# A decoder layer on one core: the next unit's projection cut into six pieces that follow the attention's stages, and four bias tiles

## The chip, the cores and the metric

The kernel runs on one core of a Trainium2 chip. The core has a matrix engine (PE; the weight loads that precede its matmuls are a row of their own, PEld), a vector engine (DVE), a scalar engine (ACT) and GpSimd (POOL), each with its own instruction stream that is worked off in order; SP issues DMAs. The metric is the device time of one execution in microseconds, the median of several runs. The engines' streams are laid out ahead of time by a tile scheduler: it goes through the program as written and by priorities, puts the instructions in an order on each engine, and adds the semaphore waits.

## The reference

A layer with two kinds of attention heads on one normed input, one output projection and an MLP; sequence and model width 1024, batch 1:

```python
def token_mixer(h, ...):
    proj = h @ w_in                       # q, k, v of 4 differential heads (2 x 64) and 8 FoX heads (64), f_logit
    cum = jnp.cumsum(jax.nn.log_sigmoid(f_logit), axis=1)
    def block(args):
        ...
        sd = q.k * 64**-0.5 + t5_bias(distance)      # differential: two score maps per head
        pd = softmax(where(causal, sd, NEG))
        ad = pd[:, :, 0] - lam * pd[:, :, 1]
        od = rmsnorm(ad @ dv, subln_g) * (1.0 - lambda_init)
        sf = q.k * 64**-0.5 + cum_q - cum_k          # FoX
        of = softmax(where(causal, sf, NEG)) @ fv
        return concatenate([od, of])
def reference(x, ...):
    h = rmsnorm(x, ln_attn_pre)
    x = x + rmsnorm(token_mixer(h, ...) @ w_out, ln_attn_post)
    u = square(relu(rmsnorm(x, ln_mlp_pre) @ w_up))
    return x + rmsnorm(u @ w_down, ln_mlp_post)
```

The code above is cut and in short form; all is float32.

## The kernel before, in words

Float32 products are made of rounded parts: each operand is split into a high part (`hi`, a cast on ACT) and a low part (`lo`, the difference, on DVE or POOL), and three matmuls (hi by hi, hi by lo, lo by hi) add up in one accumulation.

*Startup.* The eight 128-row tiles of x are loaded, and `norm_transposed` (L88 to L102) norms each: a Square on ACT (L90) into a tile y, a reciprocal root (`rstd_of`, L74 to L85), a multiplication on DVE into y (L92), eight transposes on PE (L98), the high part by ACT (L100, `hh`) and the low part by DVE (L101, `hl`). The tile y has the name "bias" and two slots in all, which it shares with the attention's bias tiles; unit 0's bias is loaded into one of them at the sixth turn of the loop.

*Units.* The attention is done in eight units u: 0 to 3 are the differential heads, 4 to 7 pairs of FoX heads. `unit_project(u)` makes the unit's q, k and v. `load_w` (L113) fetches one of the three weights (128 columns, a DMA on SP), casts it on ACT (L70, `whi`) and subtracts on POOL (L71, `wlo`), two slots each. `project` (L239) does a piece of 512 rows of h: 24 matmuls (L243 to L245) into a PSUM tile "dense" (two slots), then evacuates it at high priority: q by ACT and DVE (L261, L262), k by ACT, DVE and copies between partitions on SP (L269 to L273), v by ACT (L276), four transposes on PE (L280) and high and low part `vv` on ACT and DVE (L283, L284; FoX L289, L290). A unit has three weights and two such pieces of each. Unit 0 is done in 256-row pieces between its attention's stages.

*Attention.* `unit_attention(u, ms, ...)` goes through stages: for a differential unit m = 0 to 3, for a FoX unit m = 0 to 3 with either head, thus 4 or 8 of growing width. A stage is `softmax` (L309): scores on PE (L323, mask L326 for FoX, L328), bias and row maximum in one DVE reduction (L332), exp on ACT (L338), reciprocal on DVE (L341), and the scaling, on DVE for differential heads (L346 to L348), on POOL for FoX (L352). Then `flush` issues the `attend` of the stage before: transposes of the probabilities (L379), high and low part (ACT L381, DVE L382), V matmuls (L390 to L394; FoX L398, L399), for differential heads a norm with a matmul by ones (L409), and a store to DRAM (L424).

*Order.* The main loop (L484) writes for each u: the whole `unit_project(u)`, then `bias_tiles(u)` (a 512 KB DMA; FoX units have two), then `unit_attention(u)`. Unit 7's projection is written between unit 6's m = 1 and m = 2; `split_w_out` (eight casts and subtractions of the output projection's weight, POOL L71 `wol`) and unit 7's attention follow. The scheduler mixes what is written one behind the other: the next unit's matmuls fill places of the attention before. A period in what follows is the time from one unit's first attend to the next unit's.

Of the kernel before, what the change touches and what calls it, by code (L numbers as in the profile page):

```python
# [16 lines left out]
P = 128  # L17
# [16 lines left out]
def layer_kernel(ctx, tc, x, ln_attn_pre, w_in, b_f, lam_q1, lam_k1, lam_q2, lam_k2, subln_g,  # L34
# [111 lines left out]
    def bias_tiles(u):  # L146
        if u < 4:
            tb = bp.tile([P, S], F32, name="bias", bufs=2)
            nc.sync.dma_start(tb, toeplitz(u))
            return [tb, tb]  # L150
        tiles = []
        for s in range(2):
            tb = bp.tile([P, S], F32, name="bias", bufs=2)
            nc.sync.dma_start(tb, cumd[2 * (u - 4) + s].partition_broadcast(P))
            tiles.append(tb)
        return tiles
# [7 lines left out]
    for t in range(NB + 1):  # L164
# [19 lines left out]
        if t:  # L184
            y = bp.tile([P, D], F32, name="bias", bufs=2)
            norm_transposed(xts[t - 1], g_pre, y, hh, hl, t - 1)
# [61 lines left out]

    def unit_project(u):
        diff = u < 4  # L250
        base = 128 * u if diff else 1536 + 128 * (u - 4)
        qs = [b1.tile([P, S], F32R, name=f"qs{s}") for s in range(2)]
        k1 = [b1.tile([P, S], F32R, name=f"k1{s}") for s in range(2)]
        kl = [bp.tile([P, S], F32R, name=f"kl{s}") for s in range(2)]
        vt = b1.tile([P, S], F32, name="vt", bufs=1)
        vv = bp.tile([P, NB, 256], F32R, name="vv")

# [17 lines left out]
        def evac_v(ps, cs):  # L275
            nc.scalar.copy(vt[:, cs], ps)  # L276
            t0, nt = cs.start // P, (cs.stop - cs.start) // P
            tr = ps_t.tile([P, 4, P], F32, name="tr")[:, :nt, :]
            for k in range(nt):
                nc.tensor.transpose(tr[:, k, :], vt[:, (t0 + k) * P:(t0 + k + 1) * P], ident)  # L280
            dst = vv[:, t0:t0 + nt, :]
# [11 lines left out]
        evacs = (evac_q, evac_k, evac_v)  # L293
        if u == 0:
            for c in range(4):
                for w, evac in zip(w_first, evacs):
                    project(w, evac, c, 256)
                if c == 0:
                    lam_setup()
                    tiles = (qs, k1, kl, vv, bias0)  # L300
                unit_attention(0, (c,), *tiles)
        else:
            for n, evac in enumerate(evacs):
                w = load_w(base + 512 * n)
                for c in range(2):
                    project(w, evac, c, 512)
        return qs, k1, kl, vv

# [49 lines left out]
    def attend(u, m, heads, vv, probs):  # L358
# [6 lines left out]
        for kp in range(m + 1):  # L365
# [18 lines left out]
            for n, k in enumerate(order):  # L384
# [4 lines left out]
                if diff:  # L389
                    nc.tensor.matmul(pv[:, 0, :], vv[:, k, 0:128], rh, start=start,  # L390
                                     stop=False)
                    nc.tensor.matmul(pv[:, 0, :], vv[:, k, 0:128], rl, start=False,
                                     stop=False)
                    nc.tensor.matmul(pv[:, 0, :], vv[:, k, 128:256], rh, start=False,  # L394
                                     stop=stop)
                else:
                    vs = vv[:, k, 128 * s:128 * s + 128]
                    nc.tensor.matmul(pv[:, s, :], vs, rh, start=start, stop=False)  # L398
# [37 lines left out]

    def unit_attention(u, ms, qs, k1, kl, vv, bias):
        for u, m, heads in stages(u, ms):
            probs = softmax(u, m, heads, qs, k1, kl, vv, bias)
            flush()  # L440
            waiting.append(lambda u=u, m=m, heads=heads, probs=probs: attend(u, m, heads, vv, probs))

# [40 lines left out]
    octx = ExitStack()  # L483
    for u in range(8):  # L484
        if u == 1:
            forget_gates()
        if u == 7:
            unit_attention(6, range(2), *tiles)
        proj = unit_project(u)
        if u == 7:  # L490
            hctx.close()
            wo = pool("wo", stack=octx, side="right")
            w_o = []
            unit_attention(6, (2,), *tiles)
            split_w_out(0)
            unit_attention(6, (3,), *tiles)
            split_w_out(4)
        if u == 0:
            continue
        tiles = (*proj, bias_tiles(u))  # L500
        if u == 6:
            continue
        unit_attention(u, range(4), *tiles)
    flush()
# [433 lines left out]
```

## Time and profile before

| | |
|---|---|
| median of 3 runs | 1255.13 us (1254.7 to 1255.17) |
| profiled execution's own time | 1255.45 us |
| its span | 1253.7 us |
| PE busy | 1217.9 us, 97% of the span |
| PEld busy | 1009.0 us, 80% |
| DVE, ACT, POOL busy | 865.5 (69%), 647.7 (52%), 167.8 us (13%) |
| the chain that ended last, by engine | PE 87%, DVE 5%, ACT 4%, POOL 2%, DMA 2% |
| granted PE clock | 1.00 in every stretch read |

Busy time of PE counts a matmul from its start to its modelled end; matmuls overlap, so a stretch can be 100% busy and still hold waits between starts. An engine's row in a grouped view gives how many instructions, their busy time, the mean of one, and the idle time ahead of them with what ended it.

### The profile page before, as it was taken

To read this page: it belongs to the slowest core of one execution; us is meant where nothing else is said; L and a number is where in the kernel's file an instruction comes from. 1 tells how busy PE (TensorE), PEld (TensorE's weight loads), DVE (VectorE), ACT (ScalarE), POOL (GpSimd) and SP (SyncE) were. 2 spreads that over 40 slices of the span, in tenths; PEclk is the share of its full clock that TensorE was granted. 3 is DMA by queue.
4 is the path that set the end of the run, shared out by engine and by line. 5 is a ranking of instruction groups with operands and counts; after the bars stand their busy time and mean duration, and the time that the engine had idled before them with its cause. 6 is when DMAs were issued, how large, how long until landed. Compare 5 with 4: busy or idle time off the path is not lost.

```text
span 1253.7 us, 17424 instructions
## 1 busy us (share of the span) xinstructions
PE 1217.9 (97%) x6076; PEld 1009.0 (80%) x6076; DVE 865.5 (69%) x1844; ACT 647.7 (52%) x1269; POOL 167.8 (13%) x248
## 2 busy tenths in 40 slices
PE   6899999999999998999999999999999999999997
PEld 5877888888888887788887888888888888888886
DVE  6893969695747427855588667666645784775998
ACT  5663646464646438745474554454444444444552
POOL 3011111102323218400001000000000000000100
PEclk9999999999999999999999999999999999999999
DMA  7423031312131325333404544435349963335474
GB/s 244 115 73 85 26 97 39 93 56 63 52 88 48 84 59 193 102 127 115 150 18 126 210 157 171 146 134 182 120 158 345 365 193 95 101 93 168 147 230 170
DMA packets 122524, 164.15 MB, mean 131 GB/s; under 512 B 9656, under 2 KB 80312, under 8 KB 120516
## 3 DMA queue, kind: packets, MB, share of 16 engines
q1 hardware_dynamic: 116436, 130.53, 34.6%
q0 software_dynamic: 5424, 31.46, 6.2%
q8 instruction: 48, 0.79, 0.3%
q10 hardware_dynamic: 576, 1.05, 0.2%
q14 instruction: 40, 0.33, 0.1%
HBM read 112.62 MB, written 44.35 MB: 125 GB/s over the span
## 4 chain that ended last, share of the span: by engine, by line
PE 87%; DVE 5%; ACT 4%; POOL 2%; DMA 2%; issue 1%; SPq 0%; DVEq 0%; ACTq 0%; POOLq 0%
PE dense L244 6%; PE dense L245 6%; PE dense L243 6%; PE sc L575 3%; PE sc L577 3%; PE sc L579 3%; PE tr L379 3%; PE tr L779 3%; PE tr L780 3%; PE tr L781 3%; PE dense L780 2%; PE dense L781 2%; PE tr L575 2%; PE tr L577 2%; PE dense L779 2%; PE sc L779 2%
## 5 line engine op out<-in xcount | busy, mean ns | idle before, releaser
L70 ACT CAST whi<-wraw 128x512 fp32r<-128x512 f32 (+4 forms) x167 | 126.5, 763 | 263.2 <-PE dense L244 59.0
L71 DVE TENSOR_TENSOR wlo<-wraw,whi 128x512 fp32r<-128x512 f32 (+4 forms) x144 | 116.1, 808 | 92.1 <-ACT whi L70 86.8
L243 PE MATMUL dense<-hh,whi 128*128 128x512 f32 (+1 forms) x400 | 151.2, 378 | 1.8 <-DVE qs L262 1.3
L245 PE MATMUL dense<-hh,wlo 128*128 128x512 f32 (+1 forms) x400 | 152.4, 381 | 0.0
L244 PE MATMUL dense<-hl,whi 128*128 128x512 f32 (+1 forms) x400 | 151.7, 379 | 0.1
L338 ACT ACTIVATE p<-p,nmax 128x128 f32<-128x128 f32 (+7 forms) x128 | 99.4, 778 | 30.5 <-DVE nmax L332 28.7
L332 DVE CUSTOM_DVE_ANT_0 p<-sc,bias 128x512 f32<-128x512 f32 (+3 forms) x128 | 74.2, 585 | 38.0 <-PE sc L328 30.3
L71 POOL TENSOR_TENSOR wlo<-wraw,whi 128x1024 fp32r<-128x1024 f32 x23 | 55.5, 2412 | 241.8 <-ACT whi L70 188.4
L243 PEld LDWEIGHTS dense<-hh,whi 128*128 128x128 f32 x400 | 76.2, 191 | 14.2 <-issue 1.7
L244 PEld LDWEIGHTS dense<-hl,whi 128*128 128x128 f32 x400 | 76.1, 190 | 12.4 <-DVE hl L101 0.4
L245 PEld LDWEIGHTS dense<-hh,wlo 128*128 128x128 f32 x400 | 76.1, 190 | 11.1
L382 DVE TENSOR_TENSOR pl<-tr,ph 128x512 fp32r<-128x512 f32 (+1 forms) x120 | 73.5, 630 | 9.0 <-ACT ph L381 6.1
L379 PE MATMUL tr<-ident,p 128*128 128x128 f32 x432 | 67.7, 274 | 7.6 <-POOL p L352 5.4
L323 PE MATMUL sc<-k,qs 128*128 128x512 f32 (+2 forms) x192 | 73.2, 383 | 1.3 <-DVE nmax L332 1.2
L381 ACT CAST ph<-tr 128x512 fp32r<-128x512 f32 (+1 forms) x120 | 61.9, 543 | 21.9 <-PE tr L379 16.6
L328 PE MATMUL sc<-kl,qs 128*128 128x512 f32 (+2 forms) x192 | 71.7, 376 | 1.4 <-DMA kl<-kl 1.4
L379 PEld LDWEIGHTS tr<-ident,p 128*128 128x128 f32 x432 | 50.8, 140 | 15.6 <-POOL p L352 8.0
L614 DVE TENSOR_TENSOR r<-sc,m 128x512 f32<-128x512 f32 x42 | 28.9, 689 | 40.0 <-PE sc L579 40.0
L352 POOL TENSOR_SCALAR p<-p,rs 128x128 f32<-128x128 f32 (+3 forms) x64 | 49.3, 775 | 50.3 <-DVE rs L341 43.0
L779 PE MATMUL tr<-whi 128*128 128x512 f32 x144 | 56.0, 389 | 0.0
L780 PE MATMUL tr<-wlo,whi 128*128 128x512 f32 x144 | 56.0, 389 | 0.0
L781 PE MATMUL tr<-whi,wlo 128*128 128x512 f32 x144 | 56.0, 389 | 0.0
(293 smaller groups left out, 3241.7 us busy)
## 6 DMA issues: line engine op xcount, KB each, us to landing
wraw<-ud SPq DMA_DIRECT2D x112, 256.0 KB, 2.8
ud<-sp POOLq DMA_DIRECT2D x15, 1024.0 KB, 4.6
b<-in_w_down_dram SPq DMA_DIRECT2D x48, 256.0 KB, 5.4
wraw<-in_w_in_dram SPq DMA_DIRECT2D x23, 512.0 KB, 4.1
ud<-r POOLq DMA_DIRECT2D x15, 768.0 KB, 5.2
wraw<-in_w_down_dram SPq DMA_DIRECT2D x36, 256.0 KB, 4.1
wraw<-in_w_up_dram SPq DMA_DIRECT2D x16, 512.0 KB, 4.2
k<-in_w_up_dram SPq DMA_DIRECT2D x16, 512.0 KB, 4.9
```

What stands on the lines that cost most here:

```text
L70: nc.scalar.copy(hi, src)
L71: (lo_eng or nc.vector).tensor_tensor(lo, src, hi.bitcast(F32), op=ALU.subtract)
L243: nc.tensor.matmul(ps, hi[:, kt, :], hh[:, kt, cs], start=kt == 0, stop=False)
L244: nc.tensor.matmul(ps, hi[:, kt, :], hl[:, kt, cs], start=False, stop=False)
L245: nc.tensor.matmul(ps, lo[:, kt, :], hh[:, kt, cs], start=False, stop=kt == KT - 1)
L332: nc.vector.tensor_tensor_reduce(out=pr[:, c0:c1], in0=sc[:, :c1 - c0], in1=bias[s][:, b0 + c0:b0 + c1], scale=-1.0, scalar=BIG if nmax is ...
L338: nc.scalar.activation(pr[:, :w], pr[:, :w], AF.Exp, bias=nmax, scale=-1.0, accum_out=ssum)
L379: nc.tensor.transpose(tr[:, first + n, :], probs[i][:, k * P:(k + 1) * P], ident)
L382: nc.vector.tensor_tensor(pl[:, first:], tr[:, first:], ph[:, first:].bitcast(F32), op=ALU.subtract)
L779: nc.tensor.matmul(ps[k], sh[:, cs], th, start=p == 0, stop=False)
L780: nc.tensor.matmul(ps[k], sh[:, cs], tl, start=False, stop=False)
L781: nc.tensor.matmul(ps[k], sl[:, cs], th, start=False, stop=p == NP - 1)
```

## The change

`unit_project(u)` no longer does the work for u from 1 on; it returns the tiles (lists that are filled when a piece is first issued) and six pieces: q, k, v by two halves of 512 rows. `unit_attention` takes these pieces and a count for each of its stages, and writes so many of them behind the `flush` of the stage. Unit u + 1's pieces are written in unit u's attention: for the differential units 1 to 3 with the counts 1, 1, 2, 2; for the FoX units 4 and 5 with 0, 1, 0, 1, 1, 1, 1, 1; unit 7's in the first four stages of unit 6 (m = 0 and 1) with 1, 1, 2, 2. Unit 1's own pieces follow the forget gates in one row, as before. The bias tiles of unit u + 1 are loaded ahead of unit u's attention, and "bias" has four slots. The two further tiles of 128 x 1024 float32 take 8 KiB of each partition; the program's scratch for dynamic DMAs is set to 8192 bytes.

```diff
     def bias_tiles(u):
         if u < 4:
-            tb = bp.tile([P, S], F32, name="bias", bufs=2)
+            tb = bp.tile([P, S], F32, name="bias", bufs=4)
...
         if t:
-            y = bp.tile([P, D], F32, name="bias", bufs=2)
+            y = bp.tile([P, D], F32, name="bias", bufs=4)
             norm_transposed(xts[t - 1], g_pre, y, hh, hl, t - 1)
...
         else:
-            for n, evac in enumerate(evacs):
-                w = load_w(base + 512 * n)
-                for c in range(2):
-                    project(w, evac, c, 512)
-        return qs, k1, kl, vv
+            ws = {}
+
+            def piece(n, c):
+                if c == 0:
+                    tiles_of(n)
+                    ws[n] = load_w(base + 512 * n)
+                project(ws[n], evacs[n], c, 512)
+
+            pieces = [lambda n=n, c=c: piece(n, c) for n in range(3) for c in range(2)]
+        return tiles, pieces
...
-    def unit_attention(u, ms, qs, k1, kl, vv, bias):
-        for u, m, heads in stages(u, ms):
+    def unit_attention(u, ms, qs, k1, kl, vv, bias, fill=(), counts=()):
+
+        fill = list(fill)
+        for (u, m, heads), n in zip(stages(u, ms), counts or [0] * 8):
             probs = softmax(u, m, heads, qs, k1, kl, vv, bias)
             flush()
+            for _ in range(n):
+                fill.pop(0)()
             waiting.append(lambda u=u, m=m, heads=heads, probs=probs: attend(u, m, heads, vv, probs))
...
-    for u in range(8):
-        if u == 1:
-            forget_gates()
-        if u == 7:
-            unit_attention(6, range(2), *tiles)
-        proj = unit_project(u)
...
-        tiles = (*proj, bias_tiles(u))
-        if u == 6:
-            continue
-        unit_attention(u, range(4), *tiles)
+    unit_project(0)
+    forget_gates()
+    proj, pieces = unit_project(1)
+    for piece in pieces:
+        piece()
+    tiles = (*proj, bias_tiles(1))
+    for u in range(1, 6):
+        proj, pieces = unit_project(u + 1)
+        bias = bias_tiles(u + 1)
+        unit_attention(u, range(4), *tiles, pieces,
+                       (1, 1, 2, 2) if u < 4 else (0, 1, 0, 1, 1, 1, 1, 1))
+        tiles = (*proj, bias)
+    proj, pieces = unit_project(7)
+    bias = bias_tiles(7)
+    unit_attention(6, range(2), *tiles, pieces, (1, 1, 2, 2))
...
+    unit_attention(7, range(4), *proj, bias)
...
-    nc = bacc.Bacc("TRN2", target_bir_lowering=False, num_devices=1)
+    nc = bacc.Bacc("TRN2", target_bir_lowering=False, num_devices=1,
+                   dynamic_dma_scratch_size=8192)
```

The order of the instructions at three places. First ACT in the startup, before; `bias` here is the tile y, and L90 is its Square:

```order
30 L100 CAST hh<-tr 128x4x128 x2
31 L90 ACTIVATE bias,ssq<-p 128x1024
32 L78 ACTIVATE rs_r<-ssq,eps 128x1
33 L202 ACTIVATE lam_s<-lam_s 128x2
34 L81 ACTIVATE rs_r<-rs_r 128x1
35 L338 ACTIVATE p,ssum<-p,nmax 128x256
36 L269 CAST k_419<-dense 64x256
37 L269 CAST k_420<-dense 64x256
38 L100 CAST hh<-tr 128x4x128 x2
39 L90 ACTIVATE bias,ssq<-p 128x1024
40 L276 COPY vt<-dense 128x256
41 L78 ACTIVATE rs_r<-ssq,eps 128x1
```

and after the change, where the line numbers below L180 are the same and the later ones stand 7 to 15 higher:

```order
28 L90 ACTIVATE bias,ssq<-p 128x1024
29 L268 ACTIVATE qs_417<-dense 64x256
30 L78 ACTIVATE rs_r<-ssq,eps 128x1 x2
31 L81 ACTIVATE rs_r<-rs_r 128x1 x2
32 L268 ACTIVATE qs_418<-dense 64x256
33 L100 CAST hh<-tr 128x4x128 x2
34 L90 ACTIVATE bias,ssq<-p 128x1024
35 L276 CAST k_419<-dense 64x256
36 L78 ACTIVATE rs_r<-ssq,eps 128x1
37 L81 ACTIVATE rs_r<-rs_r 128x1
38 L276 CAST k_420<-dense 64x256
39 L100 CAST hh<-tr 128x4x128 x3
```

The Squares (L90) of the last rows of x now follow one another closely, ahead of unit 0's first exps (L338 before, L353 now).

Second, ACT at the change from unit 1's attention to unit 2's, before; the k, vt and vv rows evacuate unit 2's pieces, exp (L338) of 128x128 is unit 2's first stage:

```order
195 L407 ACTIVATE tmp<-pv 128x256
196 L410 ACTIVATE dr<-tr,eps 128x256
197 L411 ACTIVATE dr<-dr 128x256
198 L70 CAST whi<-wraw 128x1024
199 L269 CAST k_2572<-dense 64x512
200 L269 CAST k_2573<-dense 64x512
201 L276 COPY vt<-dense 128x512
202 L283 CAST vv<-tr 128x4x128
203 L70 CAST whi<-wraw 128x1024
204 L276 COPY vt<-dense 128x512
205 L338 ACTIVATE p,ssum<-p,nmax 128x128 x2
206 L283 CAST vv<-tr 128x4x128
```

and after (L283 is vt, L290 vv, L353 exp, L396 ph, L422 to L426 the norm):

```order
191 L396 CAST ph<-tr 128x384
192 L353 ACTIVATE p,ssum<-p,nmax 128x896
193 L353 ACTIVATE p,ssum<-p,nmax 128x1024 x2
194 L422 ACTIVATE tmp<-pv 128x256
195 L283 COPY vt<-dense 128x512
196 L425 ACTIVATE dr<-tr,eps 128x256
197 L426 ACTIVATE dr<-dr 128x256
198 L290 CAST vv<-tr 128x4x128
199 L70 CAST whi<-wraw 128x1024
200 L283 COPY vt<-dense 128x512
201 L353 ACTIVATE p,ssum<-p,nmax 128x128 x2
202 L290 CAST vv<-tr 128x4x128
```

The k evacuations and the first half of v's have moved ahead of or among the last exps and the norm of unit 1; the last four rows, from the cast of the next weight over vt and the exps to vv, stand as before.

Third, POOL between two FoX units, before; L352 is the scaling of the probabilities, L373 and L374 clear two blocks, L71 is the low part of a projection weight:

```order
76 L352 TENSOR_SCALAR p<-p,rs 128x896
77 L352 TENSOR_SCALAR p<-p,rs 128x1024
78 L373 MEMSET ph 128x128
79 L374 MEMSET pl 128x128
80 L71 TENSOR_TENSOR wlo<-wraw,whi 128x1024 x3
81 L352 TENSOR_SCALAR p<-p,rs 128x128
82 L352 TENSOR_SCALAR p<-p,rs 128x256
83 L352 TENSOR_SCALAR p<-p,rs 128x128
84 L373 MEMSET ph 128x128
```

and after, where L367 is the scaling, within one unit's stages:

```order
69 L71 TENSOR_TENSOR wlo<-wraw,whi 128x1024
70 L388 MEMSET ph 128x128
71 L389 MEMSET pl 128x128
72 L367 TENSOR_SCALAR p<-p,rs 128x640
73 L367 TENSOR_SCALAR p<-p,rs 128x768
74 L388 MEMSET ph 128x128
75 L367 TENSOR_SCALAR p<-p,rs 128x640
76 L389 MEMSET pl 128x128
77 L367 TENSOR_SCALAR p<-p,rs 128x768
78 L71 TENSOR_TENSOR wlo<-wraw,whi 128x1024
79 L367 TENSOR_SCALAR p<-p,rs 128x896
```

The three subtractions that stood together behind a unit's widest scalings now stand apart, each between scalings of that unit.

## Rows read from the trace of the kernel before

**Rows 1.** Page, busy us of each engine (share of the span), instructions
```profile
PE 1217.9 (97%) x6076; PEld 1009.0 (80%) x6076; DVE 865.5 (69%) x1844; ACT 647.7 (52%) x1269; POOL 167.8 (13%) x248
```

**Rows 2.** Windows: stretch, length, busy PE, PEld, DVE, ACT, POOL (instructions), PEclk, DMA
```profile
15.00:76.00 61.00, 56.40 (x414) 52.15 (x414) 50.17 (x142) 37.05 (x97) 9.17 (x8) 1.00 0.46 135
...
187.10:244.70 57.60, 56.91 (x304) 47.44 (x305) 44.88 (x129) 31.88 (x70) 8.58 (x11) 1.00 0.24 65
...
365.50:429.20 63.70, 63.58 (x370) 53.38 (x369) 36.76 (x104) 35.28 (x78) 21.64 (x36) 1.00 0.25 67
429.20:471.00 41.80, 41.44 (x216) 34.41 (x215) 16.93 (x41) 16.91 (x40) 9.12 (x18) 1.00 0.22 57
471.00:522.00 51.00, 44.52 (x290) 36.04 (x289) 38.31 (x120) 41.09 (x87) 36.77 (x45) 1.00 0.45 147
```

**Rows 3.** Chain of waits: start us, length us, what held the end
```profile
179.77 0.23 PE dense L245
...
182.28 0.24 PE dense L244
...
182.59 1.05 ACT whi L70
...
186.44 0.61 DVE vv L284
...
187.09 0.66 PE tr L379 x4
...
189.26 0.12 PE pv L390
...
194.72 0.43 PE tr L409 x2
...
301.04 0.06 PE sc L326
```

**Rows 4.** PE grouped by shape, 187.0 to 244.6: busy, mean ns, idle before
```profile
L245 PE MATMUL dense<-hh,wlo 128*128 128x512 f32 x48 | 19.4, 404 | 0.0
...
L379 PE MATMUL tr<-ident,p 128*128 128x128 f32 x36 | 5.4, 274 | 0.7 <-DVE vv L284 0.7
```

**Rows 5.** PE grouped by shape, 365.5 to 429.2
```profile
L326 PE MATMUL sc<-mask_b,ident_b 128*128 128x128 bf16 x16 | 3.7, 229 | 0.0
```

**Rows 6.** Windows, the halves of two periods and two stretches of the startup
```profile
182.60:215.00 32.40, 31.71 (x184) 26.70 (x183) 30.23 (x98) 22.33 (x52) 6.19 (x10) 1.00 0.09 26
215.00:240.20 25.20, 25.20 (x123) 20.75 (x124) 14.66 (x31) 9.55 (x18) 2.39 (x1) 1.00 0.44 115
358.00:397.00 39.00, 38.88 (x253) 32.81 (x252) 29.24 (x92) 26.66 (x64) 15.33 (x30) 1.00 0.18 55
397.00:421.00 24.00, 24.00 (x116) 20.10 (x115) 7.52 (x12) 8.07 (x14) 6.34 (x6) 1.00 0.34 84
30.00:45.00 15.00, 12.36 (x99) 11.62 (x98) 10.17 (x38) 8.67 (x26) 0.00 (x0) 1.00 0.80 208
45.00:60.00 15.00, 14.28 (x105) 12.81 (x103) 14.41 (x44) 9.88 (x26) 0.00 (x0) 1.00 0.18 45
```

**Rows 7.** DVE grouped by shape, 15 to 76
```profile
L92 DVE SCALAR_TENSOR_TENSOR bias<-p,rs_r,k 128x1024 f32<-128x1024 f32 x6 | 7.7, 1282 | 0.1
```

**Rows 8.** Waits of PE, 15 to 76: us in total, times, longest
```profile
PE tr L98 <- DVE bias L92: 2.5, 3, 1.0
```

**Rows 9.** POOL grouped by shape, 365.5 to 429.2
```profile
L71 POOL TENSOR_TENSOR wlo<-wraw,whi 128x1024 fp32r<-128x1024 f32 x4 | 9.6, 2391 | 33.4 <-ACT whi L70 33.4
L352 POOL TENSOR_SCALAR p<-p,rs 128x1024 f32<-128x1024 f32 x2 | 2.2, 1125 | 1.0 <-DVE rs L341 1.0
```

**Rows 10.** Waits of PE, 471 to 522
```profile
PE tr L379 <- POOL p L352: 5.4, 6, 1.4
```

**Rows 11.** Waits of DVE, 471 to 522
```profile
DVE p L332 <- DMA bias<-cumd: 0.9, 1, 0.9
```

**Rows 12.** Page, DMA issues: engine, kind, count, KB each, us to landing
```profile
ud<-sp POOLq DMA_DIRECT2D x15, 1024.0 KB, 4.6
```

More of the change, by code (lines that the diff above doesn't have):

```diff
@@ L152, in bias_tiles @@
         for s in range(2):
-            tb = bp.tile([P, S], F32, name="bias", bufs=2)
+            tb = bp.tile([P, S], F32, name="bias", bufs=4)
             nc.sync.dma_start(tb, cumd[2 * (u - 4) + s].partition_broadcast(P))
@@ L251, in unit_project, with tiles_of @@
         base = 128 * u if diff else 1536 + 128 * (u - 4)
[L252 to L256, printed above, removed]
+        qs, k1, kl, vv, vt = ([] for _ in range(5))
+        def tiles_of(n):
+            if n == 0:
+                qs.extend(b1.tile([P, S], F32R, name=f"qs{s}") for s in range(2))
+            elif n == 1:
+                k1.extend(b1.tile([P, S], F32R, name=f"k1{s}") for s in range(2))
+                kl.extend(bp.tile([P, S], F32R, name=f"kl{s}") for s in range(2))
+            else:
+                vt.append(b1.tile([P, S], F32, name="vt", bufs=1))
+                vv.append(bp.tile([P, NB, 256], F32R, name="vv"))
         def evac_q(ps, cs):
@@ L275, in evac_v @@
         def evac_v(ps, cs):
-            nc.scalar.copy(vt[:, cs], ps)
+            nc.scalar.copy(vt[0][:, cs], ps)
             t0, nt = cs.start // P, (cs.stop - cs.start) // P
@@ L279, in evac_v @@
             for k in range(nt):
-                nc.tensor.transpose(tr[:, k, :], vt[:, (t0 + k) * P:(t0 + k + 1) * P], ident)
-            dst = vv[:, t0:t0 + nt, :]
+                nc.tensor.transpose(tr[:, k, :], vt[0][:, (t0 + k) * P:(t0 + k + 1) * P], ident)
+            dst = vv[0][:, t0:t0 + nt, :]
             if diff:
@@ L293, in unit_project @@
         evacs = (evac_q, evac_k, evac_v)
+        tiles = (qs, k1, kl, vv)
+        pieces = []
         if u == 0:
+            for n in range(3):
+                tiles_of(n)
             for c in range(4):
@@ L299, in unit_project @@
                     lam_setup()
-                    tiles = (qs, k1, kl, vv, bias0)
-                unit_attention(0, (c,), *tiles)
-        else:
-            for n, evac in enumerate(evacs):
-                w = load_w(base + 512 * n)
-                for c in range(2):
-                    project(w, evac, c, 512)
-        return qs, k1, kl, vv
+                unit_attention(0, (c,), *tiles, bias0)
+        else:
+            ws = {}
+            def piece(n, c):
+                if c == 0:
+                    tiles_of(n)
+                    ws[n] = load_w(base + 512 * n)
+                project(ws[n], evacs[n], c, 512)
+            pieces = [lambda n=n, c=c: piece(n, c) for n in range(3) for c in range(2)]
+        return tiles, pieces
     def softmax(u, m, heads, qs, k1, kl, vv, bias):
@@ L389, in attend @@
                 if diff:
-                    nc.tensor.matmul(pv[:, 0, :], vv[:, k, 0:128], rh, start=start,
+                    nc.tensor.matmul(pv[:, 0, :], vv[0][:, k, 0:128], rh, start=start,
                                      stop=False)
-                    nc.tensor.matmul(pv[:, 0, :], vv[:, k, 0:128], rl, start=False,
+                    nc.tensor.matmul(pv[:, 0, :], vv[0][:, k, 0:128], rl, start=False,
                                      stop=False)
-                    nc.tensor.matmul(pv[:, 0, :], vv[:, k, 128:256], rh, start=False,
+                    nc.tensor.matmul(pv[:, 0, :], vv[0][:, k, 128:256], rh, start=False,
                                      stop=stop)
                 else:
-                    vs = vv[:, k, 128 * s:128 * s + 128]
+                    vs = vv[0][:, k, 128 * s:128 * s + 128]
                     nc.tensor.matmul(pv[:, s, :], vs, rh, start=start, stop=False)
@@ L483, in layer_kernel @@
     octx = ExitStack()
-    for u in range(8):
-        if u == 1:
-            forget_gates()
-        if u == 7:
-            unit_attention(6, range(2), *tiles)
-        proj = unit_project(u)
[L490 to L498, printed above, removed]
-            continue
-        tiles = (*proj, bias_tiles(u))
-        if u == 6:
-            continue
-        unit_attention(u, range(4), *tiles)
+    unit_project(0)
[13 more added lines that the diff above has]
+    unit_attention(6, range(2), *tiles, pieces, (1, 1, 2, 2))
+    hctx.close()
+    wo = pool("wo", stack=octx, side="right")
+    w_o = []
+    unit_attention(6, (2,), *tiles)
+    split_w_out(0)
+    unit_attention(6, (3,), *tiles)
+    split_w_out(4)
+    unit_attention(7, range(4), *proj, bias)
     flush()
```

## The prediction

> **What bounds the kernel now.** I read the page's busy table first: PE is busy 1217.9 us, 97% of the span [rows 1]. Then the windows, stage by stage, to see where the 3% lies [rows 2]. The reader is to see that it lies in few places. From 15 to 76 us, where rows of x are still normed and transposed and unit 0 is projected and attended, PE is busy 56.40 of 61.00 us and DVE 50.17. A differential unit's period (187.10 to 244.70) has PE 56.91 of 57.60; units 1 to 3 have such a period. A FoX period (365.50 to 429.20) has 63.58 of 63.70, and there are two. From 471 to 522, the tail of the attention, PE has 44.52 of 51.00. From 522 on the change moves next to nothing.
>
> Busy PE is not PE at its peak, so I work out what a period would take if nothing were ever late, by the start-to-start steps in the chain of waits [rows 3]: 0.23 us for a dense matmul of 512 columns (179.77 to 182.28 is eleven, so 0.228), 0.12 for a V matmul of 256, 0.215 for each of two ones matmuls of the norm, 0.06 for a mask matmul; a transpose of 128 columns I take at 0.11, a score matmul of 384 at 0.17, between these. With the counts by shape (the first row of each kind stands in [rows 4, 5]) a differential period holds 3x48 = 144 dense and 24 score matmuls of 512 columns (168 x 0.228 = 38.3), 8 of 384 (1.4), 16 of 256 (1.9), 60 V matmuls (7.2), 36 + 8 transposes (4.8) and 8 ones matmuls (1.7): 55.3 us, so that about 2.3 of 57.6 are stall. A FoX period: 168 x 0.228 = 38.3, 8 of 384 columns 1.4, 16 of 256 columns 1.9, 16 mask matmuls 1.0, 80 V matmuls 9.6, 80 transposes 8.8: 61.0, so that about 2.7 of 63.7 are stall.
>
> Where in the period is it? The scheduler takes a differential period in two halves that differ [rows 6]: from 182.60 to 215.00 the attention of unit 2 is packed (DVE 30.23 of 32.40), and from 215.00 to 240.20 PE does what is left of the next projection (DVE 14.66 of 25.20, PE 25.20 of 25.20). The FoX halves read 29.24 of 39.00 and 7.52 of 24.00. The second halves hold no stall; all of it is in the first, where DVE has no room. One more piece has a name: at the change of units PE's first transposes wait 0.7 us for DVE's v low part [rows 4], which ends a row of steps on ACT and DVE from the cast at 182.59 to vv at 186.44 [rows 3]; the softmax of the new unit's first blocks stands between them.
>
> **The change, part by part.**
>
> *Bias slots, startup.* Until now y of the startup norms shares two slots with unit 0's bias, so from the sixth row of x on there is one y, and each Square waits for the transposes of the row ahead of it. With four slots the last rows' Squares and the DVE multiplication L92 move ahead. One row's L92 takes DVE 1.28 us [rows 7]; two of them, 2.6 us, leave the stretch of 45 to 60, where DVE is busy 14.41 of 15.00, for 30 to 45, where it has 10.17 of 15.00 [rows 6] and so 4.8 us free. PE's waits for L92 in 15 to 76 are 2.5 us in three [rows 8]. I take 1.5 us off, nearly two of the three L92 waits. Bounds: PE is idle 4.6 us in this stretch [rows 2], and no more can go; on the other side an L92 that is put ahead of a softmax reduction can hold it up by its own 1.28, so +1.3.
>
> *Pieces in the stages, differential units (3 periods).* No matmul, cast or DMA is added; 144 dense matmuls of 33 us now lie with the stage whose DVE work runs beside them. Within each period DVE's 45 us spread over 57.6 (78%) rather than 93% and 58%. The name-bearing wait at the change of units stays: ACT's rows around it (cast, vt, exps of the new unit, vv) stand as before. So of 2.3 us 0.7 stay, and of the other 1.6 I take a third, 0.5 per period, 1.5 in all, since the last stage (the widest softmax and two v pieces) remains as dense for DVE as the packed half was. Bounds: all 2.3 x 3 = -6.9; and, if the whole period came to stall at the rate of the packed half now, 2.3 x 57.6/32.4 = 4.1, so +1.8 x 3 = +5.4.
>
> *Pieces in the stages, FoX units (2 periods).* Here DVE has 37 of 63.7 and the stages of 8 are short, so a piece beside six of them leaves more room: I take 1.25 of 2.7 per period, 2.5 in all. Every weight of q, k or v takes a POOL subtraction of 2.39 us with it, which used to stand in a bunch and now stands between the probability scalings of up to 1.1 us [rows 9]. I cost it at nothing: POOL is busy 21.64 of 63.70 [rows 2], and a scaling's transposes come one stage, some 8 us, later. If that cover is gone, see the POOL rival. Bounds: -2.7 x 2 = -5.4, and +4.8, one such subtraction in each period that PE waits out.
>
> *Queues.* SP issues the same loads; the bias loads go ahead of the k copies, and the weight loads between them. A weight load that waits for its slot now holds the k copies and the mixed-head stores behind it on SP. The k copies are wanted only in the next unit, the stores in the output projection: nothing. ACT's cast waits for the last matmul of an earlier piece; what stands behind it there is mostly the evacuation of that same piece: nothing.
>
> *Unit 6 and the tail.* Unit 7's pieces lie in unit 6's first four stages, -0.3 (the window of 429.20 to 471.00 has 0.36 us of idle PE [rows 2]). In the tail POOL's order is kept, and PE's 5.4 us behind the scalings with it [rows 10]; the 0.9 us for which a reduction waited on its bias load goes [rows 11], but POOL ends last there: -0.2, bounds -0.9 and +2.4, one subtraction of POOL more ahead of a scaling.
>
> *Scratch.* POOL's descriptor scratch is set to 8192, which frees the room of the two bias tiles. It serves POOL's transfers alone; the 15 largest land 4.6 us after their issue [rows 12], and I cost the smaller scratch at nothing, since their issues lie microseconds apart. The Trainium skill (SBUF — State Buffer, SBUF size table) has that scratch as a carve-out of 16 KiB for POOL's descriptor ring; it names no price for a smaller one, and no trace here shows one.
>
> The sum: -1.5 -1.5 -2.5 -0.3 -0.2 = -6.0 us against the profiled execution's own 1255.45, so 1249.45. That execution stands 0.32 above the median of 1255.13, so the forecast is **1249.1**, and its own range 1245 to 1252.5.
>
> A rule of the Trainium skill that speaks for more: where the most contended engine changes over time, interleaving the regimes may help (Perfetto Trace Analysis, Optimization Strategy). The trace has such regimes [rows 6]; by the rule alone all the stall would go. The same page (Identifying the Most-Contended Engine) judges PE by its weight loads' busy share and not by matmuls'. Here that share is 82% both in the half with no stall (20.75 of 25.20 [rows 6]) and in the whole period (47.44 of 57.60 [rows 2]), so by it too there is little to be had in a period, and the sum stays as it is.
>
> **The rivals.**
>
> *All the stall of the attention goes*. DVE's share of 78% speaks for it, the last stage and the unit change against it. -6.9 - 5.4 - 1.5 = -13.8: about 1241.
>
> *Nothing moves.* The scheduler already mixes the projection with the packed attention, one dense matmul at a time, and keeps what is left for the end; PE has the same instructions, and the named wait at the unit change stays. Then the stall is that of pipelined waits within a stage and no filler takes it away; only the startup gains: -1, about 1254.3.
>
> *Slower: POOL's subtraction ahead of a scaling.* In the FoX periods and in unit 6 POOL gets nine such (3 units x 3) between scalings, in order. Each waits for ACT's cast, which waits for the last matmul of a piece; if the cast comes over 8 us after the scaling's own sum is ready, PE's transposes wait. What that costs is to be seen in the tail, where eight like subtractions of split_w_out stand between scalings: PE waits 5.4 us for the scalings [rows 10] and is idle 51.00 - 44.52 = 6.5 us in all [rows 2], 0.8 a subtraction. 9 x 0.8 = 7.2 in place of the FoX gain of 2.5 makes 1249.1 + 2.5 + 7.2 = 1258.8. Against it: POOL sits idle 33.4 us ahead of these subtractions in one period [rows 9]. The point from which it decides is a scaling that ends later than PE's last matmul of the stage before.
>
> *The scratch is too small* and POOL's stores of the later part wait. Were each of the 15 late by a tenth of its 4.6 us with PE behind it, 15 x 0.46 = 7 us would be lost: 1256; with the trace's silence I give it little.
>
> **How the numbers follow.** Forecast 0.50; all stall gone 0.12; nothing moves 0.20; POOL 0.15; scratch 0.03. A measurement of this kernel can tell about 0.2%, 2.5 us, from no change: faster is below 1252.6, slower above 1257.6. Faster then has 0.50 + 0.12 = 0.62, same 0.20 + 0.03 = 0.23, slower 0.15. The range is from 1243, which leaves out most of the first rival (0.08), to 1259, which leaves out half of the POOL rival (0.08). It takes in the bound of the startup on either side and about half of the differential periods' bounds; all bounds at once would need every term wrong the same way.
>
> **What would show it.** Right: in the windows the two halves of a period have like DVE shares (75 to 80% of each), periods of about 57.1 and 62.4 us, PE's waits for L92 at 1 us or less, the wait for vv still at each unit change, POOL's waits at the scalings no longer than now. Wrong: a new wait of PE for the p scaling between 300 and 430 (the POOL rival), periods of 57.6 and 63.7 as before (nothing moves), waits of the ud stores after 522 (scratch).

## The result: slower by half a percent, and the profile after

The changed kernel takes 1261.74 us (1260.17 to 1263.2) against 1255.15; the ratio is 1.0053 with the interval 1.0035 to 1.007. Forecast were 1249.1 and a range that ended at 1259. The profiled execution's span is 1259.2 us.

PE is as busy as before by its share; it has no more work and more busy time (page, after; [rows 1]):

```profile
PE 1222.4 (97%) x6076; PEld 1006.3 (80%) x6076; DVE 871.1 (69%) x1844; ACT 652.2 (52%) x1269; POOL 166.3 (13%) x248
```

To place the loss I take as marks the last transposes at each change of units: in the order both kernels have them there. Before, these stand at 127.00, 184.67, 242.27, 300.00, 365.30, 429.04 and 473.30 us, and the attention's very last at 540.30; after at 125.39 and on as the left column shows. First the windows after the change (units 1, 2, 4, 5, 6, the tail; unit 3's, 59.45, is like unit 2's), then the windows before that [rows 2] does not have:

```profile
125.39:184.64 59.25, 57.89 (x306) 47.16 (x305) 46.41 (x129) 32.79 (x70) 8.47 (x12) 1.00 0.24 63
184.64:243.95 59.31, 57.90 (x306) 47.12 (x305) 46.49 (x129) 32.78 (x70) 8.47 (x12) 1.00 0.25 63
...
303.40:369.19 65.79, 65.78 (x380) 53.96 (x379) 38.14 (x107) 36.02 (x79) 21.56 (x36) 1.00 0.25 65
369.19:433.96 64.77, 64.67 (x369) 52.41 (x367) 36.96 (x102) 35.60 (x78) 21.45 (x36) 1.00 0.25 66
433.96:479.29 45.33, 45.04 (x233) 35.82 (x232) 18.23 (x46) 18.41 (x42) 9.34 (x18) 1.00 0.20 53
479.29:546.40 67.11, 60.45 (x400) 49.62 (x399) 52.99 (x158) 52.23 (x111) 43.14 (x58) 1.00 0.44 130
```

```profile
300.00:365.30 65.30, 65.08 (x380) 54.05 (x379) 37.36 (x107) 35.82 (x79) 21.78 (x36) 1.00 0.24 65
365.30:429.04 63.74, 63.62 (x371) 53.42 (x370) 36.76 (x104) 35.32 (x78) 21.68 (x36) 1.00 0.25 67
429.04:473.30 44.26, 43.90 (x231) 36.43 (x230) 17.52 (x42) 18.11 (x42) 9.28 (x18) 1.00 0.21 54
473.30:540.30 67.00, 60.46 (x403) 50.13 (x401) 53.07 (x158) 52.27 (x111) 43.91 (x58) 1.00 0.47 146
```

The reader is to see: up to the first mark 1.6 us are gained (127.00 to 125.39). Each differential period loses 1.6 to 1.7 (59.25 to 59.45 against 57.60 to 57.73), 5.0 in all. The FoX periods lose 0.5 and 1.0, unit 6 loses 1.1; the tail (67.11 against 67.00) loses nothing, and the long rest up to the span's end gains 0.6 (1259.2 - 546.4 = 712.8 against 1253.7 - 540.3 = 713.4). -1.6 + 5.0 + 1.5 + 1.1 + 0.1 - 0.6 = +5.5, the difference of the spans; the medians differ by 6.6.

The differential periods show a wait that the kernel before did not have. PE's waits after, from 120 to 300 us:

```profile
PE sc L338 <- DVE nmax L347: 2.1, 3, 0.7
PE tr L394 <- DVE vv L291: 2.1, 3, 0.7
```

The second is that of [rows 4]. The first is new, once in each period: scores that wait for a score tile, which DVE's reduction holds. What DVE did just then, in unit 2 (timeline of DVE, then of POOL, then of PE):

```profile
206.96 0.68 DVE L269 SCALAR_TENSOR_TENSOR qs<-dense,qs 64x512 fp32r<-64x512 f32 x1
207.68 1.36 DVE L427 TENSOR_TENSOR tmp<-dr 128x256 f32<-128x256 f32 x1
208.96 0.68 DVE L347 CUSTOM_DVE_ANT_0 p<-sc,bias 128x512 f32<-128x512 f32 x1
```

```profile
206.36 2.40 POOL L71 TENSOR_TENSOR wlo<-wraw,whi 128x1024 fp32r<-128x1024 f32 x1 [15.54 <-PE tr L394]
```

```profile
209.70 0.50 PE L338 MATMUL sc<-k,qs 128*128 128x512 f32 x1 [0.71 <-DVE nmax L347]
```

L427 squares the norm's root, 128x256. It takes 0.42 us elsewhere; here it takes 1.36 and ends 0.28 after POOL's weight subtraction does. The reduction behind it is late by that, and PE's scores with it. The wait that I knew has the same cause, as the timelines before show (DVE, then POOL):

```profile
185.13 0.98 DVE L346 TENSOR_TENSOR c1s<-rs,nlam 128x1 f32<-128x1 f32 x1
```

```profile
183.71 2.38 POOL L71 TENSOR_TENSOR wlo<-wraw,whi 128x1024 fp32r<-128x1024 f32 x1 [9.01 <-ACT whi L70]
```

A product of 128x1, which takes 0.15 us elsewhere, took 0.98, up to 0.02 after POOL's end at 186.09. Beside the same subtraction DVE's reductions, reciprocals, and products that read one operand from PSUM ran at their usual length in both traces (0.68 to 0.69 us for a reduction of 512 columns and for the low part of q). The Trainium skill (SBUF — State Buffer, Who interferes with whom) has the rule: a DVE instruction with two inputs in SBUF contends with a GpSimd instruction that reads SBUF, and the one that comes second waits the first out. The traces agree: 0.98 for 0.15, and 1.31 to 1.36 for 0.42.

So theory 1: the change moved POOL's subtraction to where it meets a second of DVE's two-operand products. Theory 2: DVE has no room in the stages into which the pieces went, or PE pays for changing between kinds of matmul, of which the order has 79 in a differential period against 67.

### The profile page after: what moved, and what is told of

Its sections match the earlier page's. It is cut to its first block, busy times and chain, and to the rows that moved or that the text cites. A ratio compares the mean times of both kernels' runs of the same rounds, so it can differ in the third digit from the quotient of the medians.

```text
span 1259.2 us, 17426 instructions
## 1 busy us (share of the span) xinstructions
PE 1222.4 (97%) x6076; PEld 1006.3 (80%) x6076; DVE 871.1 (69%) x1844; ACT 652.2 (52%) x1269; POOL 166.3 (13%) x248
## 4 chain that ended last, share of the span: by engine, by line
PE 63%; DVE 2%; DMA 2%; ACT 2%; POOL 1%; issue 1%; DVEq 0%; ACTq 0%; POOLq 0%; SPq 0%
PE sc L597 3%; PE sc L601 3%; PE sc L599 3%; PE tr L801 3%; PE tr L803 3%; PE tr L802 3%; PE dense L802 2%; PE sc L801 2%; PE dense L801 2%; PE dense L803 2%; PE sc L802 2%; PE sc L803 2%; PE dense L491 2%; PE dense L489 2%; PE tr L597 2%; PE dense L490 2%
## 5 line engine op out<-in xcount | busy, mean ns | idle before, releaser
L71 DVE TENSOR_TENSOR wlo<-wraw,whi 128x512 fp32r<-128x512 f32 (+4 forms) x144 | 116.1, 808 | 91.6 <-ACT whi L70 91.2
L353 ACT ACTIVATE p<-p,nmax 128x128 f32<-128x128 f32 (+7 forms) x128 | 99.5, 778 | 36.8 <-DVE nmax L347 36.1
L71 POOL TENSOR_TENSOR wlo<-wraw,whi 128x1024 fp32r<-128x1024 f32 x23 | 55.5, 2412 | 233.6 <-ACT whi L70 218.1
L396 ACT CAST ph<-tr 128x512 fp32r<-128x512 f32 (+1 forms) x120 | 61.7, 543 | 27.4 <-PE tr L394 22.9
L338 PE MATMUL sc<-k,qs 128*128 128x512 f32 (+2 forms) x192 | 72.6, 379 | 3.1 <-DVE nmax L347 3.1
L367 POOL TENSOR_SCALAR p<-p,rs 128x128 f32<-128x128 f32 (+3 forms) x64 | 48.4, 759 | 89.0 <-DVE rs L356 65.3
```

The costliest lines, as they stand in the source:

```text
L71: (lo_eng or nc.vector).tensor_tensor(lo, src, hi.bitcast(F32), op=ALU.subtract)
L353: nc.scalar.activation(pr[:, :w], pr[:, :w], AF.Exp, bias=nmax, scale=-1.0, accum_out=ssum)
```

## The experiments

All but e13 were timed side by side with the kernel before, whose median was then 1255.37 to 1255.62; ratios are to it, with their 95% intervals.

**e1, the squaring on ACT** (changed kernel):

```diff
-            nc.vector.tensor_tensor(tmp, r, r, op=ALU.mult)
+            nc.scalar.activation(tmp, r, AF.Square)
```

> The changed kernel with the norm's squaring (tmp = r*r, L427) on ACT instead of DVE. Theory 1, POOL holds DVE: in units 1 to 3 this squaring ran beside POOL's weight subtraction and took 1.31 to 1.36 us in place of 0.42, and PE's scores waited 0.7 us for a reduction behind it. Then three such stalls go: 3 x 0.85 = 2.6 us, 1261.7 to about 1259.1, and no score wait of 0.7 us stays in units 1 to 3. Theory 2, DVE has no room in the stages that take two pieces: moving 0.42 us off DVE per norm shortens each of the three waits by 0.42 at most, 1.3 us, to 1260.4 or more, and the waits stay visible at half their length.

1257.85 us, 1.0020 (1.0011 to 1.0029). Units 1 and 2 by the same marks, and all of PE's waits from 120 to 300 us:

```profile
122.58:181.04 58.46, 57.76 (x306) 47.08 (x305) 44.12 (x125) 34.33 (x74) 8.47 (x12) 1.00 0.24 64
181.04:239.56 58.52, 57.82 (x307) 47.00 (x306) 44.18 (x125) 34.32 (x74) 8.48 (x12) 1.00 0.25 64
```

```profile
PE tr L394 <- DVE vv L291: 2.0, 3, 0.7
```

The wait for the reduction is gone whole, and 0.8 us of each period with it, as theory 1 has it. The first mark came 2.8 us earlier as well (122.58 against 125.39), which I had not expected. It is not a held squaring: in unit 0 the three squarings ahead of the mark ran at 0.42 us in the changed kernel too. What is gone there is one wait of PE's scores for a copy of k's low part, which the changed kernel has and e1 has not; why it went with this edit is not shown:

```profile
PE sc L343 <- DMA kl<-kl: 2.2, 1, 2.2
```

By the marks 2.8 + 2.4 = 5.2 us are gained and in the median 3.9; most of the rest was lost behind unit 6, whose mark stands 5.0 us earlier (474.25 in e1), where I did not follow it. In e1's period 0.9 us of the loss is left (58.5 against 57.6).

**e2, the slots alone; e3 and e4, pieces in the differential or in the FoX stages only.** e2 is the kernel before with `bufs=4` for "bias" and the scratch of 8192; in e3 and e4 the loop writes, for the other units,

```diff
-        unit_attention(u, range(4), *tiles, pieces,
-                       (1, 1, 2, 2) if u < 4 else (0, 1, 0, 1, 1, 1, 1, 1))
+            unit_attention(u, range(4), *tiles)
+            for piece in pieces:
+                piece()
```

> The kernel before with four bias slots and the 8192-byte scratch, and nothing else: the projection and the bias loads stand where they stood. By the landmarks of the two traces (last forget-gate matmul at 89.7 before, 88.1 after) the startup gains 1.6 us: 1255.15 - 1.6 = 1253.5. If the smaller scratch cost anything after 522 us, the time would be above 1255.2 minus 1.6 by that; the traces have 705.6 us from the last transposes of the attention to the end before and 705.0 after, so I expect nothing.

> The changed kernel with pieces in the stages of units 1 to 3 only; in units 4 to 6 the six pieces stand behind the attention's stages in one row, as before. If the landmarks of the traces add up (startup -1.6, three differential periods +1.7 each): 1255.15 - 1.6 + 5.1 = 1258.7. If the loss of the FoX units is a consequence of the late start they inherit and not of their own pieces, it stays and the time is 1261 or more.

> The changed kernel with pieces in the stages of units 4 to 6 only; in units 1 to 3 the six pieces stand in one row as before. If the landmarks add up (startup -1.6, FoX units +0.5 and +1.0, unit 6 +1.0): 1255.15 - 1.6 + 2.5 = 1256.0. If the FoX pieces cost nothing by themselves: 1253.5.

e2: 1254.02, 0.9990 (0.9982 to 0.9999). e3: 1259.12, 1.0033 (1.0021 to 1.0046). e4: 1256.02, 1.0007 (0.9998 to 1.0016). The parts add up as expected: the slots gain 1.4, the scratch costs nothing that can be seen, the differential pieces cost 5.1 (1259.12 - 1254.02), the FoX pieces 2.0 (1256.02 - 1254.02). e3 and e4 also keep the changed kernel's earlier bias loads, so these are in both numbers.

**e5, c1s on ACT in the kernel before; e6, squaring and c1s on ACT in the changed kernel:**

```diff
-                nc.vector.tensor_tensor(c1s, inv[1], nlam, op=ALU.mult)
+                nc.scalar.mul(c1s, inv[1], nlam)
```

> The kernel before, with the softmax's factor c1s (128x1, L346) made on ACT and nothing else moved by hand. At each change of units 1 to 3 this product ran 0.98 us in place of 0.15 beside POOL's weight subtraction, and PE's transposes waited 0.7 us for the v low part behind it. Theory 1 (POOL holds DVE's two-input operations): the three waits go, 3 x 0.7 to 0.85 = 2.1 to 2.5 us, 1255.4 to about 1253.1. Rival (the wait at the unit change is the latency of the softmax chain, whoever computes c1s): at most 0.15 each, 1254.9 or more.

> The changed kernel with the squaring and c1s on ACT: theory 1 takes 3 x 0.75 more off the run with the squaring alone, 1257.85 to about 1255.5, and no wait of PE for the v low part of 0.7 us stays in units 2 to 4. By the rival it stays near 1257.5.

e5: 1254.02, 0.9989 (0.9981 to 0.9998), a time between the two that were named, and not gained where it was expected: PE's wait for vv is gone, but another stands in its place, and the periods are longer than before (unit 1: 58.02 us against 57.67). The gain lies ahead of the first mark (125.02 against 127.00), where I did not follow it. The window of e5's unit 1, and the new wait from 120 to 300 us:

```profile
125.02:183.04 58.02, 57.03 (x307) 47.22 (x305) 46.13 (x121) 33.56 (x78) 8.56 (x12) 1.00 0.24 64
```

```profile
PE pv L390 <- DVE rs L341: 2.3, 3, 0.8
```

e6: 1259.41, 1.0035 (1.0021 to 1.0049), a miss. Both runs show why when DVE's products are grouped from 120 to 300 us; first e5, then e6, the norm's last product (dr times tmp, 0.42 us when alone):

```profile
L416 DVE TENSOR_TENSOR dr<-dr,tmp 128x256 f32<-128x256 f32 x12 | 14.7, 1226 | 0.2
```

```profile
L431 DVE TENSOR_TENSOR dr<-dr,tmp 128x256 f32<-128x256 f32 x12 | 8.3, 691 | 0.4
```

With c1s off DVE the order shifted, and the next product with two operands in SBUF met the subtraction: (1226 - 420) x 12 = 9.7 us of DVE in e5, and 3.2 in e6, where PE waited for reductions again:

```profile
PE sc L338 <- DVE nmax L347: 2.7, 3, 0.9
```

The rival for e5 (the latency of the softmax chain) is not borne out either: with c1s made elsewhere the whole wait for vv went, not 0.15 us of it.

**e9, all three freed.** To e6 this adds that the norm's correction is kept in the second half of the PSUM tile that holds the mean square (`tp`), so the last product has one operand there:

```diff
-            nc.vector.tensor_tensor(r, r, tmp, op=ALU.mult)
+            nc.vector.tensor_tensor(r, tp, r, op=ALU.mult)
```

> The changed kernel with the squaring and c1s on ACT, and the norm's correction kept in PSUM so that its last product (L431, dr times tmp) has only one operand in SBUF. In the run with the first two alone that product had taken over the wait for POOL: 1.45 to 1.51 us in place of 0.43, three times. Theory 1: no product of c1s or of the norm is held any more, and what was expected there comes now: 1257.85 - 2.3 = about 1255.5, with no wait of PE for a reduction of 0.7 us or more in units 1 to 3. Rival (the run with both was slower since ACT, with two steps more in its queue, became late): 1259 or more.

1253.62, 0.9987 (0.9978 to 0.9996), 1.9 lower than expected: below the kernel before, and 8.1 us below the changed one, with the pieces where the change put them. PE has no wait of its own from 120 to 300 us, and the product is at its length (DVE grouped; windows of units 1 and 2):

```profile
L432 DVE TENSOR_TENSOR dr<-tr,dr 128x256 f32<-128x256 f32 x12 | 5.1, 424 | 0.3
```

```profile
124.28:181.48 57.20, 57.20 (x306) 47.16 (x305) 43.33 (x117) 36.48 (x82) 8.46 (x12) 1.00 0.24 65
181.48:238.71 57.23, 57.23 (x306) 47.20 (x305) 43.38 (x117) 36.51 (x82) 8.47 (x12) 1.00 0.25 65
```

**e8 and e10, late pieces** (e1 with other counts): 0, 0, 2, 4 in units 1 to 3 (e8), and in e10 also in unit 6, with 0, 0, 0, 0, 0, 0, 2, 4 in units 4 and 5.

> The changed kernel with the squaring on ACT, and in units 1 to 3 the six pieces in the last two stages (0, 0, 2, 4) instead of 1, 1, 2, 2. Theory 2 now says: what is left of the loss per differential period (58.5 against 57.6) is paid at PE's changes between kinds of matmul, of which the order has 67 a period before, 78 in the changed kernel with the squaring on ACT, and 69 here: 3 x 0.8 = 2.4 us less, 1257.85 to about 1255.5. If what is left comes from DVE's work of the pieces in the wide stages, this puts more of it there: 1258 or more.

> The changed kernel with the squaring on ACT and the pieces late in every unit: 0, 0, 2, 4 in units 1 to 3 and 6, and 0, 0, 0, 0, 0, 0, 2, 4 in units 4 and 5. The order has 90, 83 and 27 changes of matmul kind in the periods of units 4, 5 and 6, against 95, 89 and 40 with pieces in every stage. Theory 2 (what is left of the loss is paid at these changes, 0.1 us each by the run with late pieces in units 1 to 3): 24 fewer, 1253.6 to about 1251.2. If the FoX units' loss has to do with POOL's subtractions between the scalings or with DVE's and ACT's work beside the pieces in the widest stages, it stays or grows: 1253.6 or more.

e8: 1253.60, 0.9986 (0.9977 to 0.9995), lower than expected. e10: 1251.43, 0.9968 (0.9955 to 0.9980), as expected. e8's unit 1 in the windows, with c1s still held in it:

```profile
124.00:181.42 57.42, 56.74 (x307) 47.36 (x305) 43.47 (x125) 33.45 (x74) 8.57 (x12) 1.00 0.24 65
```

So the place of the pieces was worth another microsecond a period: with four pieces in the widest stage DVE was not the worse for it, which takes "no room in the wide stages" out. POOL's hold is not what went here: c1s is as long in e8 as in e1 (0.258 us in the mean), and PE's wait for vv is the same in both (2.0 us in three). The count of changes between kinds of matmul fitted well, and so I measured it.

**e13, PE alone.** The layer is left out whole; the kernel runs matmuls in several orders and copies PSUM to the output.

> No layer at all: the output is a copy of some PSUM contents. PE alone, on data that is there from the start: 48 dense matmuls of 512 columns in a row (after 240 for warming), 48 V matmuls of 256, the two alternating one by one and four by four, 48 transposes, and dense and transposes alternating one by one and four by four. No wait on another engine. If a change of matmul kind costs by itself (theory 2, 0.03 to 0.1 us each by the periods), 48 dense and 48 V one by one take 96 x 0.03 to 96 x 0.1 = 3 to 9 us more than 48 x 0.228 + 48 x 0.119 = 16.7 us. If it does not, all orders take 16.7 us, and dense with transposes 48 x (0.228 + 0.109) = 16.2 us; then what is left of the loss is waits for other engines.

It ran once. Windows of its blocks: 48 dense; 48 V; these two one by one; 48 transposes; dense and transposes one by one; dense and V four by four.

```profile
62.71:73.59 10.88, 10.88 (x50) 9.01 (x49) 0.00 (x0) 0.00 (x0) 0.00 (x0) 1.00 0.00 0
73.59:79.34 5.75, 5.75 (x50) 5.75 (x48) 0.00 (x0) 0.00 (x0) 0.00 (x0) 1.00 0.01 3
79.34:96.31 16.97, 16.97 (x99) 14.72 (x98) 0.00 (x0) 0.00 (x0) 0.00 (x0) 1.00 0.00 0
96.30:101.46 5.16, 5.16 (x50) 5.16 (x49) 0.00 (x0) 0.00 (x0) 0.00 (x0) 1.00 0.02 3
101.46:117.91 16.45, 16.45 (x100) 13.13 (x98) 0.00 (x0) 0.00 (x0) 0.00 (x0) 1.00 0.00 0
117.91:134.81 16.90, 16.90 (x98) 14.78 (x97) 0.00 (x0) 0.00 (x0) 0.00 (x0) 1.00 0.00 1
```

In a row 10.88 + 5.75 = 16.63 us, one by one 16.97: 0.34 us for some 95 changes, 0.004 each. With transposes 16.45 against 16.04, the same. Four by four, with a quarter of the changes, it is 16.90, so even these 0.004 us are an upper bound. That half of theory 2 falls: twelve changes more are 0.05 us at most, not 0.9, and its forecast for e10 came out by luck. What a late place spares in the differential periods therefore stays open.

**e14, the FoX units' subtractions on DVE** (e4 with `split` on `nc.vector` for units 5 to 7):

> The run with pieces in the stages of units 4 to 6 only (1256.02), with the low parts of units 5 to 7's weights subtracted on DVE instead of POOL (9 of 1.3 us or so on DVE for 2.39 on POOL). If the FoX units' loss of 2.5 us against the undivided projection with the same slots (1254.0) comes from POOL's subtractions between the scalings, it goes: 1254.0 or less. If it comes from where the pieces stand on PE, it stays: about 1256.

1256.79, 1.0011 (1.0002 to 1.0020): without these subtractions on POOL the FoX units are no faster. The edit gives DVE nine subtractions in their place, which could hide a small gain; but from unit 4 to 6 PE's weight loads wait for POOL's scalings 0.9 us in e4 against 0.8 in e2, so little is there to be hidden. Windows of units 5 and 6 in e2 (undivided), e4 (the change's counts) and e10 (late), and in each from unit 4 to 6 the wait of PE's weight loads for the high parts of the probabilities:

```profile
364.10:427.90 63.80, 63.66 (x371) 53.49 (x370) 36.81 (x105) 35.42 (x79) 21.81 (x36) 1.00 0.25 67
427.90:472.10 44.20, 43.81 (x230) 36.41 (x228) 17.36 (x45) 18.09 (x44) 9.70 (x18) 1.00 0.21 54
```

```profile
PEld pv L398 <- ACT ph L381: 1.3, 4, 0.5
```

```profile
363.80:428.50 64.70, 64.60 (x368) 52.38 (x367) 37.09 (x104) 35.59 (x78) 21.47 (x36) 1.00 0.25 66
428.50:473.70 45.20, 44.91 (x232) 35.77 (x231) 17.86 (x45) 18.35 (x44) 9.82 (x18) 1.00 0.20 53
```

```profile
PEld pv L413 <- ACT ph L396: 3.4, 11, 0.5
```

```profile
360.50:424.10 63.60, 63.47 (x371) 53.34 (x370) 36.67 (x105) 35.64 (x78) 21.78 (x36) 1.00 0.24 67
424.10:468.60 44.50, 44.18 (x232) 36.39 (x230) 17.52 (x45) 17.92 (x44) 9.69 (x18) 1.00 0.21 54
```

```profile
PEld pv L413 <- ACT ph L396: 1.9, 5, 0.6
```

The loss of 0.9 and 1.0 goes with waits for ACT of some 0.3 us each that rise by 2.1 us and fall again: where a stage's dense matmuls stand apart from its transposes and V matmuls, fewer of them lie between a transpose and the V matmul that needs ACT's cast of it. That fits units 5 and 6 in size; no run tested it alone, and unit 4's loss of 0.5 us stays with late pieces too (65.80 in e10 against 65.30 in e2).

**Versions without a held product: e7, e11, e12.** e7 is e2 with squaring and c1s on ACT; e11 is e10 with all three products freed as in e9; e12 is e2 with the same three freed.

> The kernel before with the four slots, and the squaring and c1s on ACT, the projection undivided. If the parts add up: 1254.0 (slots) - 2.3 (three unit changes) = 1251.7, and about 1 us less if the squaring on ACT shortens unit 0 as it did in the changed kernel (its forget gates ended 2.8 us earlier there). It would beat both kernels.

> Late pieces in every unit, and the squaring, c1s and the norm's last product freed of POOL's hold. If the two theories hold and add up: 1251.2 - 2.3 = about 1248.9, below the best so far (1251.3, undivided projection with slots, squaring and c1s on ACT). If the pieces give nothing that the undivided projection does not have: 1251.3.

> The kernel before with the four slots, and with the squaring, c1s and the norm's last product freed of POOL's hold as in the run with late pieces (1250.07), the projection undivided. If the division into late pieces gives nothing by itself, the two are equal: 1250 to 1251.3 (the run with undivided projection and the first two freed had 1251.31 and no held product in units 1 to 3). If late pieces gain by themselves as the change meant, this one is 2 us or more slower: 1252 or more.

e7: 1251.31, 0.9969 (0.9957 to 0.9980). e11: 1250.07, 0.9957 (0.9944 to 0.9969), a microsecond above what was expected. e12: 1255.04, 0.9996 (0.9987 to 1.0005), which by the words of its expectation speaks for late pieces; but more than half of its loss against e7 is a wait that e7, undivided as well, does not have. e7 and e11, and e10 above, lie 4 to 5.5 us below the kernel before. The windows of unit 1 in e7, e11 and e12, and e12's new wait from 120 to 300 us:

```profile
124.35:181.14 56.79, 56.69 (x307) 47.21 (x305) 41.86 (x117) 34.82 (x82) 8.55 (x12) 1.00 0.24 66
```

```profile
123.54:180.47 56.93, 56.93 (x307) 47.53 (x305) 42.47 (x117) 35.30 (x82) 8.53 (x12) 1.00 0.25 65
```

```profile
124.93:183.04 58.11, 57.12 (x307) 47.18 (x305) 43.30 (x117) 34.76 (x82) 8.55 (x12) 1.00 0.24 64
```

```profile
PE pv L390 <- DVE mo L418: 2.1, 3, 0.8
```

With no product held, the differential period is 56.8 undivided (e7), 56.9 with late pieces (e11), 57.2 with the change's (e9). e12's 58.1 has a wait of another kind: V matmuls for the one pv tile, which the norm's last step frees. Between the best of each sort, e7 and e11, the intervals overlap; that dividing the projection gains anything is not shown.

## Why the prediction was wrong, point by point

**Startup, -1.5: right in size.** The marks give 1.6; the slots alone gave 1.4 by the medians, with an interval of 0.1 to 2.3 (e2). The waits that the step names tell only a part of it: PE's for L92, 2.5 us in three [rows 8], are still 1.8 in two, and not the 1 us or less that was to show the step right:

```profile
PE tr L98 <- DVE bias L92: 1.8, 2, 0.9
```

**Differential periods, -0.5 each: wrong, +1.6 to +1.7.** The step that failed is "of the other 1.6 I take a third". It took an evened-out load of DVE for shorter waits of PE, and it gave the moved POOL subtractions no price in these periods. The load was evened out as meant, from 93% and 58% to 76% and 79% (DVE in windows of unit 2 after the change):

```profile
182.60:215.00 32.40, 30.99 (x167) 24.72 (x166) 24.73 (x78) 18.78 (x44) 5.80 (x8) 1.00 0.15 42
215.00:243.50 28.50, 28.50 (x150) 23.70 (x149) 22.58 (x56) 15.59 (x29) 3.18 (x4) 1.00 0.34 84
```

In place of the gain came a squaring that runs 0.9 us longer beside POOL's subtraction, and a wait of PE's scores of 0.7 us behind it; with the squaring on ACT the period is 0.8 us shorter (e1). That the wait for vv stays came true, but I had misread it, and so missed the sign. I took it for the end of a row of softmax steps and left out the step that made it: between the rows that I chose at 182.59 and 186.44 [rows 3] the chain has DVE's c1s at 185.13, a 128x1 product of 0.99 us. A row whose duration is six times that of its like was the sign that POOL and DVE hold each other up. I then weighed POOL's moved subtractions by what stands behind them on POOL, in the FoX units, and not by what DVE does beside them.

The other half of the loss, 0.9 us a period, is only narrowed down. It goes when the pieces stand late, with c1s still held (57.4, e8); with all held products freed, 0.4 of it is left where the change put the pieces (57.2 in e9 against 56.8 undivided in e7). By which wait it comes about is open.

**The bound of that term** (+1.8 a period, "the rate of the packed half") held the outcome by its size, but for another reason, and so by luck.

**FoX periods, -1.25 each, and unit 6, -0.3: wrong, +0.5, +1.0 and +1.1.** The step "so a piece beside six of them leaves more room" took DVE's free share for what PE waits on. What the runs show in its place is that the stall of units 5 and 6 rises and falls with the waits of PE's weight loads for ACT's casts, between transposes and V matmuls (1.3 us undivided, 3.4 with the change's counts, 1.9 with late pieces); that a filler helps only where it lies between these two would fit, but is not shown. Late pieces gave 2.2 us back (e10 against e8).

**Tail and scratch, about nothing: right.** 67.11 us against 67.00, and 712.8 against 713.4 from there to the span's end. In the tail that is in part luck: PE's waits for POOL's scalings, which were to stay, fell from 5.4 us [rows 10] to 3.5, and waits for ACT's casts (1.1 us) and DVE came up instead.

```profile
PE tr L394 <- POOL p L367: 3.5, 5, 1.1
```

**The rivals.** The POOL rival named the right instruction and the wrong victim: its price made 1258.8, but by PE's waits for POOL's scalings, of which the changed kernel has none from 303 to 434 us and fewer in the tail. "All the stall goes" fell: DVE's load was evened out as meant, and the periods grew. The Trainium skill (Perfetto Trace Analysis, Optimization Strategy) says only that interleaving such regimes may help; with these counts it did not. None of the signs that I had listed was the one that came, a wait of PE's scores for a DVE reduction.

## What to carry to other kernels

When a change moves a POOL instruction that reads SBUF, list what DVE will do beside it, not only what POOL does behind it: three DVE products with both operands in SBUF ran here until POOL was done or a little longer, even one of 128x1. Group a line by duration and look for single instructions several times as long as their like; then look at what POOL does beside them. Curing one may hand the wait to the next product (e5, e6), so free all of them, by ACT or by an operand in PSUM, or move the POOL work, and compare arrangements only after that.

## What the runs showed of the hardware that I had not expected

- On PE alone a change between dense matmuls and V matmuls or transposes costs 0.004 us at most, in the orders tried (e13).
- A DVE product of two SBUF operands beside POOL's subtraction of 2.39 us ran until that ended or up to 0.3 us longer: 0.98 us in place of 0.15 with 0.96 left of it, 1.36 in place of 0.42 with 1.08 left.
- Three edits that each leave PE's work as it is moved the time by 8.1 us (1261.74 to 1253.62, e9), more than the whole change did (6.6).
